# Gate and up of a SwiGLU feed-forward as seven block products, with summed weights made by accumulating DMAs

## The chip, the cores and the metric

The kernel runs on one NeuronCore of one Trainium2 chip. The metric is the device time of one execution in microseconds (us), lower is better. The core has five engines that run side by side, each in its own program order: TensorE (PE, matmuls; PEld is its weight load), VectorE (DVE), ScalarE (ACT), GpSimd (POOL) and SyncE (SP, which here only issues DMAs).

## What is computed

Two transformer blocks run one after the other on 256 tokens of 1024 channels, all in float32. The first has four layers (convolution, pooling, differential attention, convolution), the second two layers with a token mixer each. Eight SwiGLU feed-forwards (FFN) lie between them, one in each layer of the first block and two in each layer of the second:

```python
def _swiglu(xn, w_gate, w_up, w_down):
    return (jax.nn.silu(xn @ w_gate) * (xn @ w_up)) @ w_down
```

`xn` is 256 x 1024 (normalised), `w_gate` and `w_up` are 1024 x 2816, `w_down` is 2816 x 1024. The mixers between the feed-forwards are not touched by the change.

## The kernel before

**Split numbers.** A float32 operand is held as two fp32r tiles, a rounded high part and the low rest. `mm3` (L184 to L191) makes one 128-row product with three matmuls: high times high (L187), high times low (L188), low times high (L189). A weight block is loaded by SP from HBM into a slot of pool `r8` (L113), ACT rounds it into a second slot (L134) and DVE subtracts to get the low part in a third (L135), each in two halves of 128x1024. There are 19 such slots.

**The planner.** All weight loads stand in one list of pieces of up to 1 MB (`add`), in the order of their use. Every `mm3` ends with `tick`, which records at most one half of a split (`split_step`) and any delayed tasks that are due. `need(i)` forces the splits up to piece i, `done` frees the two slots of a piece, and `load_step` issues the next load when a slot is free. So the order on all engines comes from counting ticks (three matmuls each) while the program is recorded.

**The feed-forward.** `ffn` (L337) works on six chunks of the 2816 columns, five of 512 and one of 256. `gate_up(c, h)` takes one half h of the tokens (128) against gate and up of a chunk: for each of the two, eight blocks of 128 channels accumulate in a PSUM bank. ACT then takes SiLU of the gate (L368), DVE multiplies by up (L369), PE transposes the result four times (L375), ACT and DVE split it (L196, L197), and `down(c, h)` accumulates it against `w_down` into two banks per half. `chain` at the end of each half takes the norm, adds to x and transposes x for the next part (`post`, `scale_of`, `to_T`).

```python
    def tick(self):
        self.ticks += 1
        self.split_step()
        for t in list(self.tasks):
            if t in self.tasks and t[0] <= self.ticks:
                self.step(t)
```

Of the kernel before, what the change touches and what calls it, by code (L numbers as in the profile page):

```python
# [27 lines left out]
ORD = "VQKvco"  # L28

# [20 lines left out]
class Core:  # L50
    def __init__(self, ctx, tc, I, out):
# [21 lines left out]
        self.raw, self.hl, self.xt = {}, {}, {}  # L73
        self.raw_max = 3
        self.spare = 2
        self.hold = 0
        self.rr = {}
# [17 lines left out]
    def add(self, *srcs):  # L95

        self.pieces.append(srcs)
        return len(self.pieces) - 1

    def view(self, t, i):  # L100
        srcs = self.pieces[i]
        kt, n = srcs[0].shape[1], sum(s.shape[2] for s in srcs)
        return t[:, 0:kt * n].rearrange("p (k n) -> p k n", k=kt)

    def load_step(self, most=10 ** 9):
        while self.n_dma < most and self.n_dma < len(self.pieces) and len(self.r8.free) > self.spare and len(self.raw) < self.raw_max:
# [8 lines left out]
            self.raw[i] = t  # L115
            self.n_dma += 1

    def split_step(self, force=False, eng=None):
        i = self.n_split
        if i >= len(self.pieces):  # L120
            return False
        if self.sub == 0:
# [3 lines left out]
            if i not in self.raw:  # L126
                return False
            self.hl[i] = (self.r8.get(), self.r8.get())
            self.live += 1
        hi, lo = (self.view(t, i) for t in self.hl[i])  # L130
        k = lo.shape[1]
        sl = slice(0, k // 2) if self.sub == 0 else slice(k // 2, k)
        raw = self.view(self.raw[i], i)[:, sl]
        self.nc.scalar.copy(out=hi[:, sl], in_=raw)  # L134
        (eng or self.nc.vector).tensor_tensor(out=lo[:, sl], in0=raw, in1=hi[:, sl].bitcast(F32), op=ALU.subtract)  # L135
        self.sub += 1
        if self.sub == 2:
            self.sub = 0
            self.r8.put(self.raw.pop(i))
            self.n_split += 1  # L140
            self.load_step()
        return True

    def need(self, i):
        self.cur = max(self.cur, i)
        while self.n_split <= i:
            assert self.split_step(force=True), ("no buffer for piece", i, self.n_dma, self.n_split, len(self.raw), self.raw_max, len(self.r8.free), self.sub)
        return tuple(self.view(t, i) for t in self.hl[i])
# [35 lines left out]
    def mm3(self, out, x, w, first, last, tick=True):  # L184

        mm = self.nc.tensor.matmul
        mm(out=out, lhsT=x[0], rhs=w[0], start=first, stop=False)  # L187
        mm(out=out, lhsT=x[0], rhs=w[1], start=False, stop=False)  # L188
        mm(out=out, lhsT=x[1], rhs=w[0], start=False, stop=last)  # L189
        if tick:  # L190
            self.tick()  # L191
# [64 lines left out]
    def scale_of(self, h):  # L256
# [5 lines left out]
        def rest():  # L262
            r = self.sb.tile([128, 4], F32, tag=f"rr{h}", name=f"rr{h}", bufs=2)
            self.rstd(sx, 2, EPS, r)
            self.rr[h] = r[:, 1:2]
        return rest

    def to_T(self, h, gT, rest, late):
# [12 lines left out]
        for n, z in enumerate(zs):  # L281
            dst = [t[:, 0:2048].rearrange("p (k t) -> p k t", k=8)[:, 4 * n:4 * n + 4, h * 128:(h + 1) * 128] for t in self.xT]
            self.split(dst[0], dst[1], z.rearrange("p (k t) -> p k t", k=4))
            self.f2.put(z)
# [5 lines left out]
        self.spawn(last(), 3 if late else 0)  # L290
        yield
# [18 lines left out]
    def start(self, h, nxt, wait=None, late=False):  # L310
        rest = (lambda: self.scale_of(h)()) if late else self.scale_of(h)
# [4 lines left out]
        else:  # L316
            self.hold += 1
            self.xt[h] = self.spawn(self.to_T(h, self.gT, rest, late), 6 if wait is None else wait)


    def plan_ffn(self, wg, wu, wd):

        G, Dn = [], []
# [3 lines left out]
        for c in range(6):  # L327
            lo = c * 512
            if c < 5:
                G.append([self.add(w[:, 4 * q:4 * q + 4, lo:lo + 512]) for w in (gk, uk) for q in range(2)])  # L330
                Dn.append([self.add(dk[:, 4 * c + 2 * q:4 * c + 2 * q + 2, :]) for q in range(2)])
            else:
                G.append([self.add(gk[:, 4 * q:4 * q + 4, lo:lo + 256], uk[:, 4 * q:4 * q + 4, lo:lo + 256]) for q in range(2)])
                Dn.append([self.add(dk[:, 20:22, :])])
        return G, Dn

    def ffn(self, plan, half, nxt):  # L337
        G, Dn = plan
        self.limit = 6
# [3 lines left out]
        hT, tt = {}, {}  # L343

        def gate_up(c, h):
# [22 lines left out]
            self.nc.scalar.activation(out=s[:, 0:n], in_=gb, func=ACTF.Silu, scale=rr[h])  # L368
            self.nc.vector.scalar_tensor_tensor(out=s[:, 0:n], in0=ub, scalar=rr[h], in1=s[:, 0:n], op0=ALU.mult, op1=ALU.mult)  # L369
            self.ps.put(*banks)  # L370

            def T():
                b = self.ps.get()
                for j in range(n // 128):
                    self.nc.tensor.transpose(out=b[:, j * 128:(j + 1) * 128], in_=s[:, j * 128:(j + 1) * 128], identity=self.ident)  # L375
                self.f2.put(s)
                hT[c, h] = (self.r2.get(), self.r2.get())
                self.split(hT[c, h][0][:, 0:n], hT[c, h][1][:, 0:n], b[:, 0:n])
                self.ps.put(b)
                yield  # L380
            tt[c, h] = self.spawn(T(), 11 if c < 5 else 3)
# [25 lines left out]
        for c in range(5):  # L407
            if c == 4 and nxt == "pool":
                self.band = self.r8.get(F32)
                self.nc.sync.dma_start(out=self.band[:, 0:1568], in_=self.band_dram)  # L410
            gate_up(c, 0)
            if c:
                down(c - 1, 1)
            else:
# [1028 lines left out]
```

## Time and profile before

| | |
|---|---|
| median of 3 runs | 2160.31 us (2160.1 to 2162.17) |
| the profiled execution's own time | 2164.11 us |
| its span in the profile | 2162.3 us |
| mean granted TensorE clock | 0.997 |
| busy share of the span: PE, DVE, ACT, POOL | 99%, 57%, 49%, 4% |
| moved by DMA | 383.73 MB, 177 GB/s |

The profile is one execution, seen by engine. Busy time of an engine is the union of its instructions' times; matmuls are pipelined, so a matmul's duration (0.39 us) is longer than the step from one start to the next, and the step is what counts. "idle before" says how long an engine stood idle ahead of a group and which instruction ended that.

### The profile page before, as it was taken

Reading aid. Unit: us, or ns where it says so; the run is one execution under the profiler, and the core shown is the slowest. Engines: PE = TensorE matmul, PEld = TensorE weight load, DVE = VectorE, ACT = ScalarE, POOL = GpSimd, SP = SyncE. Lnnn points to the kernel's source line nnn. Section 1 sums busy time; section 2 is a strip of 40 time slices with the busy share of each in tenths; the row PEclk is TensorE's granted clock in tenths of the full one; section 3 lists DMA queues with packets and bytes.
Section 4 is the critical chain, followed back from the end, with each engine's and each line's share of the span. In section 5 each row is a group of like instructions: output and inputs, shape, how many; then the busy total and the mean of one; then the engine's idle time right before and its main releaser. Section 6 shows DMA issues by size and latency. Waiting matters only on the chain.

```text
span 2162.3 us, 24820 instructions
## 1 busy us (share of the span) xinstructions
PE 2138.5 (99%) x9845; PEld 1729.2 (80%) x9845; DVE 1237.1 (57%) x1664; ACT 1066.4 (49%) x1566; POOL 82.2 (4%) x130
## 2 busy tenths in 40 slices
PE   9999999999999999999999999999999999999998
PEld 6878877887888888888888887878888888787886
DVE  6655475546665456655464554785456446477454
ACT  5554454444664435553454446764435345676342
POOL 1000010000010000000000001000000001000000
PEclk9999999999999999999999999999999999999999
DMA  8555545455454554554654554354554645345541
GB/s 295 188 201 197 190 166 179 171 196 186 137 197 163 200 189 161 210 179 156 213 189 170 193 181 142 118 193 167 196 191 150 214 171 171 128 165 175 175 176 59
DMA packets 175620, 383.73 MB, mean 177 GB/s; under 512 B 10428, under 2 KB 29116, under 8 KB 175504
## 3 DMA queue, kind: packets, MB, share of 16 engines
q1 hardware_dynamic: 172592, 372.04, 50.2%
q0 software_dynamic: 2624, 9.58, 1.2%
q8 instruction: 77, 1.26, 0.2%
q10 hardware_dynamic: 288, 0.52, 0.1%
q14 instruction: 39, 0.32, 0.0%
HBM read 380.28 MB, written 1.84 MB: 177 GB/s over the span
## 4 chain that ended last, share of the span: by engine, by line
PE 93%; DVE 3%; ACT 2%; issue 1%; POOL 1%; DMA 0%; SPq 0%; POOLq 0%; DVEq 0%; ACTq 0%
PE ps L189 29%; PE ps L188 29%; PE ps L187 29%; PE ps L206 2%; PE ps L375 2%; ACT r L134 1%; DVE r L135 1%; PE ps L1042 1%; ACT c_junk L220 1%; PE ps L687 0%; PE ps L732 0%; PE ps L783 0%; PE ps L1016 0%; ACT f L1029 0%; DMA r<-in_conv_w_in_dram 0%
## 5 line engine op out<-in xcount | busy, mean ns | idle before, releaser
L187 PE MATMUL ps<-r,r 128*128 128x512 f32 (+2 forms) x2816 | 1129.5, 401 | 2.6 <-ACT r L196 1.7
L188 PE MATMUL ps<-r,r 128*128 128x512 f32 (+2 forms) x2816 | 1108.1, 394 | 2.5 <-POOL r L135 1.4
L189 PE MATMUL ps<-r,r 128*128 128x512 f32 (+2 forms) x2816 | 1109.5, 394 | 0.1
L135 DVE TENSOR_TENSOR r<-r,r 128x1024 fp32r<-128x1024 f32 (+1 forms) x701 | 815.1, 1216 | 147.0 <-ACT r L134 140.3
L134 ACT CAST r<-r 128x1024 fp32r<-128x1024 f32 x702 | 686.0, 1041 | 194.7 <-PE ps L188 166.8
L189 PEld LDWEIGHTS ps<-r,r 128*128 128x128 f32 (+1 forms) x2816 | 528.2, 188 | 127.1 <-DVE r L197 3.8
L188 PEld LDWEIGHTS ps<-r,r 128*128 128x128 f32 (+1 forms) x2816 | 529.3, 188 | 119.3 <-DVE r L135 3.0
L187 PEld LDWEIGHTS ps<-r,r 128*128 128x128 f32 (+1 forms) x2816 | 529.3, 188 | 118.8 <-ACT r L196 2.2
L369 DVE SCALAR_TENSOR_TENSOR f<-ps,rr,f 128x512 f32<-128x512 f32 (+1 forms) x96 | 67.8, 706 | 458.6 <-PE ps L189 434.4
L196 ACT CAST r<-ps 128x512 fp32r<-128x512 f32 (+1 forms) x108 | 59.9, 555 | 456.2 <-PE ps L375 448.1
L197 DVE TENSOR_TENSOR r<-ps,r 128x512 fp32r<-128x512 f32 (+1 forms) x108 | 70.2, 651 | 189.4 <-ACT r L196 189.4
L368 ACT ACTIVATE f<-ps,rr 128x512 f32<-128x512 f32 (+1 forms) x96 | 62.6, 653 | 156.9 <-PE ps L189 156.8
L216 POOL TENSOR_TENSOR st<-st,c_mhalf 128x1 f32<-128x1 f32 x28 | 15.9, 569 | 1575.7 <-DVE st L215 1574.9
L220 ACT ACTIVATE c_junk<-x 128x512 bf16<-128x512 f32 x56 | 35.3, 631 | 51.3 <-DVE x L253 50.2
L375 PEld LDWEIGHTS ps<-c_ident,f 128*128 128x128 f32 x352 | 44.4, 140 | 13.1
L375 PE MATMUL ps<-c_ident,f 128*128 128x128 f32 x352 | 54.0, 272 | 0.0
L277 DVE TENSOR_TENSOR f<-ps,c_pre 128x512 f32<-128x512 f32 x52 | 33.8, 687 | 29.5 <-PE ps L206 29.3
L196 ACT CAST r<-f 128x512 fp32r<-128x512 f32 x52 | 31.7, 621 | 26.1 <-DVE f L277 26.0
L253 DVE SCALAR_TENSOR_TENSOR x<-f,st,x 128x512 f32<-128x512 f32 x56 | 39.6, 749 | 2.5 <-POOL st L216 0.9
L245 DVE TENSOR_TENSOR f<-ps,gn 128x512 f32<-128x512 f32 x52 | 35.5, 684 | 6.4 <-ACT c_junk L220 6.4
L220 ACT ACTIVATE c_junk<-ps 128x512 bf16<-128x512 f32 x52 | 31.0, 596 | 15.2 <-PE ps L189 14.4
L197 DVE TENSOR_TENSOR r<-f,r 128x512 fp32r<-128x512 f32 x52 | 35.6, 722 | 4.6 <-ACT r L196 2.5
(177 smaller groups left out, 749.3 us busy)
## 6 DMA issues: line engine op xcount, KB each, us to landing
r<-in_ffn_w_in_dram SPq DMA_DIRECT2D x80, 1024.0 KB, 5.2
r<-in_ffn_w_down_dram SPq DMA_DIRECT2D x44, 1024.0 KB, 5.0
r<-in_ffn_w_out_dram SPq DMA_DIRECT2D x44, 1024.0 KB, 5.1
r<-in_ffn_w_gate_dram SPq DMA_DIRECT2D x40, 1024.0 KB, 5.1
r<-in_ffn_w_up_dram SPq DMA_DIRECT2D x40, 1024.0 KB, 5.1
r<-in_mix_w_in_dram SPq DMA_DIRECT2D x28, 1024.0 KB, 5.1
r<-in_conv_w_in_dram SPq DMA_DIRECT2D x22, 1024.0 KB, 5.3
r<-in_attn_w_qkv_dram SPq DMA_DIRECT2D x12, 1024.0 KB, 5.2
```

The costliest lines, as they stand in the source:

```text
L134: self.nc.scalar.copy(out=hi[:, sl], in_=raw)
L135: (eng or self.nc.vector).tensor_tensor(out=lo[:, sl], in0=raw, in1=hi[:, sl].bitcast(F32), op=ALU.subtract)
L187: mm(out=out, lhsT=x[0], rhs=w[0], start=first, stop=False)
L188: mm(out=out, lhsT=x[0], rhs=w[1], start=False, stop=False)
L189: mm(out=out, lhsT=x[1], rhs=w[0], start=False, stop=last)
L196: self.nc.scalar.copy(out=hi, in_=src)
L197: self.nc.vector.tensor_tensor(out=lo, in0=src, in1=hi.bitcast(F32), op=ALU.subtract)
L206: self.nc.tensor.transpose(out=b[:, j * 128:(j + 1) * 128], in_=src[:, j * 128:(j + 1) * 128], identity=self.ident)
L220: self.nc.scalar.activation(out=self.junk[:, 0:src.shape[-1]], in_=src, func=ACTF.Square, scale=scale, accum_out=acc)
L368: self.nc.scalar.activation(out=s[:, 0:n], in_=gb, func=ACTF.Silu, scale=rr[h])
L369: self.nc.vector.scalar_tensor_tensor(out=s[:, 0:n], in0=ub, scalar=rr[h], in1=s[:, 0:n], op0=ALU.mult, op1=ALU.mult)
L375: self.nc.tensor.transpose(out=b[:, j * 128:(j + 1) * 128], in_=s[:, j * 128:(j + 1) * 128], identity=self.ident)
```

## The change

Chunks 1 to 4 of each feed-forward (`SUMS`) no longer take `gate_up`. With two halves of the tokens, two halves of the input channels, and gate and up as the two column blocks, gate and up of a chunk are a 2x2 by 2x2 block product, which before was eight products of 12 matmuls. `seven(c)` takes seven: a11·b11, a12·b21, s1·t1, s2·t2, s4·b22, s3·t3, a22·t4. b11 and b21 are the upper and lower channel halves of gate, b12 and b22 those of up. The sums are t1 = b11 + b12, t2 = t1 + b22, t4 = t2 + b21 and t3 = b22 + b12. The sums of x (s1 to s4) are made once per feed-forward (`x_sums`, a task that follows the second `to_T`).

A summed block is made in place: when ACT and DVE have split the raw block, POOL issues a DMA that adds the next block from HBM onto the raw slot, and the sum is split in turn. In chunk 1 alone t1 is summed by DVE from two loaded blocks. A split of a summed block is not recorded earlier than 14 ticks (42 matmuls) after its DMA, unless it is forced. Loads, sums and splits of a chunk stand in a new order (`plan_ffn`), and each half's two `down` parts of the chunk before stand between the products.

```diff
+    def add_sums(self, b11, b12, b21, b22, loaded):
+        at = {}
+        def take(name):
+            src, more = {"b11": (b11, b12), "t1": (b11, b22), "t2": (b11, b21), "t4": (b11, None),
+                         "b22": (b22, b12), "t3": (b22, None), "b21": (b21, None)}[name]
...
+    def flush(self, keep=0):
+        while len(self.lows) > keep:
+            lo, raw, hi, eng, i, last = self.lows.popleft()
+            eng.tensor_tensor(out=lo, in0=raw, in1=hi.bitcast(F32), op=ALU.subtract)
+            if last:
+                self.n_low = i + 1
+                src, more, _ = self.units[i]
+                if more is None:
+                    self.r8.put(self.raw.pop(src))
+                elif more is not IN_PLACE:
+                    self.nc.gpsimd.dma_start(out=self.view(self.raw[src], src), in_=more, accum_op=ALU.add)
+                    self.due[src] = self.ticks + 14
...
         if self.sub == 0:
-            if not force and (self.hold or i > self.cur + self.ahead or self.live >= self.limit or len(self.r8.free) < 2):
+            if not force and (self.hold or i > self.cur + self.ahead or self.live >= self.limit or self.due.get(src, 0) > self.ticks
+                              or len(self.r8.free) < 2 + self.reserve):
...
+            if first is not None:
+                a, b = (self.view(self.raw[n], src) for n in (src, first))
+                self.nc.vector.tensor_tensor(out=a, in0=a, in1=b, op=ALU.add)
...
+        for c in SUMS:
+            if c > 1:
+                factors(c, "b21")
+            factors(c, "b22", "t2")
+            down(c - 1, 0)
+            factors(c + 1, "b11")
+            factors(c, "t3")
+            down(c - 1, 1)
+            factors(c, "t4")
+            factors(c + 1, "t1")
...
+        def seven(c):
...
+            product(X, "b11", "a11", True)
+            e1 = self.spawn(copy("1", X), 2)
+            product(Z, "b21", "a12", True)
+            self.join(e1)
+            e2 = self.spawn(gate0(), 2)
+            Y = self.ps.get()
+            product(Y, "t1", "s1", True)
+            e3 = self.spawn(copy("5", Y), 2)
+            product(X, "t2", "s2")
+            e4 = self.spawn(copy("2", X), 2)
+            down(c - 1, 0, (0,))
+            down(c - 1, 1, (0,))
+            self.join(e2, e3)
+            product(Y, "b22", "s4")
+            self.join(e4)
+            e5 = self.spawn(up0(), 2)
+            product(X, "t3", "s3")
+            e6 = self.spawn(up1(), 1)
+            down(c - 1, 0, (1,))
+            down(c - 1, 1, (1,))
+            self.join(e5, e6)
+            product(X, "t4", "a22")
```

`copy` is an ACT copy of a PSUM bank to SBUF, after which the bank goes on accumulating; `gate0`, `up0` and `up1` are one DVE addition of a bank and such a copy each, the first with SiLU on ACT behind it, the second with the DVE multiplication; `gate1` is SiLU and multiplication of the second half. Other edits: DVE's subtraction is recorded one split later than ACT's rounding, the negated row scale is kept for both halves, and live splits in a feed-forward may be 7 (6 before).

The order of POOL in the fifth feed-forward before: between its last small steps and those of the next part it has nothing (L216 are powers for the norms, L228 loads a gain, L902 belongs to the mixer).

```order
L216 TENSOR_TENSOR rr0_9186<-rr0_9186,c_mhalf_65 128x1
L216 TENSOR_TENSOR st4_9201<-st4_9201,c_mhalf_65 128x1
L228 DMA gn_1_9207<-in_norm_gain_2_dram 128x1024
L902 MEMSET r8_9_9233 128x768
L216 TENSOR_TENSOR rr1_9275<-rr1_9275,c_mhalf_65 128x1
```

The same engine now, from the start of the fifth feed-forward (L164 is the accumulating DMA, `r8_9_8420` is block b11 of chunk 2, `r8_11_8518` is b22 of chunk 2).

```order
L295 DMA gn_0_8220<-in_norm_gain_2_dram 128x1024
L283 TENSOR_TENSOR rr1_8263<-rr1_8263,c_mhalf_65 128x1
L164 DMA r8_7_8098<-in_ffn_w_in_2_dram 128x4x512
L164 DMA r8_11_8351<-in_ffn_w_in_2_dram 128x4x512
L164 DMA r8_7_8098<-in_ffn_w_in_2_dram 128x4x512
L164 DMA r8_9_8420<-in_ffn_w_in_2_dram 128x4x512 x2
L164 DMA r8_11_8518<-in_ffn_w_in_2_dram 128x4x512
L164 DMA r8_9_8420<-in_ffn_w_in_2_dram 128x4x512
```

There are 15 such DMAs of 1 MB in a feed-forward, three onto one block in turn.

The order of ACT in the same feed-forward, at the end of chunk 1 and the start of chunk 2 (`r8_13_8660` is the high part of t2 of chunk 2, L556 the SiLU of chunk 1's second half, L533 a copy of a bank, L263 the split of a transposed result).

```order
L201 CAST r8_13_8660<-r8_9_8420 128x1024
L556 ACTIVATE f2_1_8663<-ps_5_8415,rr1_8263 128x512
L201 CAST r8_13_8660<-r8_9_8420 128x1024
L201 CAST r8_15_8682<-r8_10_8554 128x1024 x2
L533 COPY f2_6_8690<-ps_3_8651 128x512
L263 CAST r2_0_8701<-ps_1_8696 128x512
```

The rounding of a summed block stands directly ahead of a SiLU that PE's next transposes depend on.

The order of DVE at the start of the same feed-forward (L380 to L387 are the sums of x, L187 the sum t1 of chunk 1, L157 the low part of a weight block, L510 the product of gate and up in chunk 0).

```order
L264 TENSOR_TENSOR r8_1_8281<-f2_9_8250,r8_16_8280 128x512
L157 TENSOR_TENSOR r8_14_8302<-r8_11_8273,r8_15_8301 128x1024 x2
L387 SCALAR_TENSOR_TENSOR f2_3_8192<-f2_6_8185,f2_3_8192 128x512
L264 TENSOR_TENSOR r8_1_8281<-f2_6_8185,r8_16_8280 128x512
L510 SCALAR_TENSOR_TENSOR f2_5_8329<-ps_2_8226,rr0_8198,f2_5_8329 128x512
L264 TENSOR_TENSOR r8_1_8281<-f2_3_8192,r8_16_8280 128x512
L187 TENSOR_TENSOR r8_7_8098<-r8_7_8098,r8_3_8118 128x2048
L157 TENSOR_TENSOR r8_12_8355<-r8_7_8098,r8_17_8354 128x1024 x2
```

The sums of x stand among the splits, and the first accumulating DMA (onto `r8_7_8098`) can only go out behind the last row here.

## Rows read from the trace of the kernel before

**Rows 1.** The page: busy time by engine, and the chain that ended last.
```profile
PE 2138.5 (99%) x9845; PEld 1729.2 (80%) x9845; DVE 1237.1 (57%) x1664; ACT 1066.4 (49%) x1566; POOL 82.2 (4%) x130
...
PE 93%; DVE 3%; ACT 2%; issue 1%; POOL 1%; DMA 0%; SPq 0%; POOLq 0%; DVEq 0%; ACTq 0%
PE ps L189 29%; PE ps L188 29%; PE ps L187 29%; PE ps L206 2%; PE ps L375 2%; ACT r L134 1%; DVE r L135 1%; PE ps L1042 1%; ACT c_junk L220 1%; PE ps L687 0%; PE ps L732 0%; PE ps L783 0%; PE ps L1016 0%; ACT f L1029 0%; DMA r<-in_conv_w_in_dram 0%
```

**Rows 2.** Busy time in four feed-forwards (us and instructions, clock, DMA share, GB/s).
```profile
925.20:1115.60 190.40, 190.40 (x854) 154.55 (x853) 103.15 (x112) 84.94 (x111) 3.82 (x5) 1.00 0.54 185
1115.60:1306.00 190.40, 190.33 (x854) 154.04 (x852) 101.61 (x111) 82.14 (x110) 6.62 (x10) 1.00 0.54 185
1452.60:1642.30 189.70, 189.70 (x848) 153.65 (x848) 101.79 (x110) 84.97 (x111) 2.74 (x5) 1.00 0.53 183
1642.30:1832.00 189.70, 189.70 (x848) 153.59 (x847) 101.61 (x111) 82.12 (x110) 6.16 (x9) 1.00 0.54 186
```

**Rows 3.** Timeline of PE in a feed-forward: start, us, instruction.
```profile
119.69 0.39 PE L188 MATMUL ps<-r,r 128*128 128x512 f32 x1
...
127.53 0.39 PE L189 MATMUL ps<-r,r 128*128 128x512 f32 x1
127.77 0.60 PE L375 MATMUL ps<-c_ident,f 128*128 128x128 f32 x4
128.12 0.47 PE L187 MATMUL ps<-r,r 128*128 128x512 f32 x1
...
133.05 0.39 PE L188 MATMUL ps<-r,r 128*128 128x512 f32 x1
...
138.42 0.39 PE L187 MATMUL ps<-r,r 128*128 128x512 f32 x1
```

**Rows 4.** Groups of instructions, whole span: busy us, mean ns, idle before.
```profile
L135 DVE TENSOR_TENSOR r<-r,r 128x1024 fp32r<-128x1024 f32 (+1 forms) x701 | 815.1, 1216 | 147.0 <-ACT r L134 140.3 <-PE ps L189 4.1
L134 ACT CAST r<-r 128x1024 fp32r<-128x1024 f32 x702 | 686.0, 1041 | 194.7 <-PE ps L188 166.8 <-DVE r L135 21.7 <-DMA r<-in_conv_w_in_dram 6.2
...
L197 DVE TENSOR_TENSOR r<-ps,r 128x512 fp32r<-128x512 f32 (+1 forms) x108 | 70.2, 651 | 189.4 <-ACT r L196 189.4
L369 DVE SCALAR_TENSOR_TENSOR f<-ps,rr,f 128x512 f32<-128x512 f32 (+1 forms) x96 | 67.8, 706 | 458.6 <-PE ps L189 434.4 <-ACT f L368 24.2
L368 ACT ACTIVATE f<-ps,rr 128x512 f32<-128x512 f32 (+1 forms) x96 | 62.6, 653 | 156.9 <-PE ps L189 156.8
...
L245 DVE TENSOR_TENSOR f<-ps,gn 128x512 f32<-128x512 f32 x52 | 35.5, 684 | 6.4 <-ACT c_junk L220 6.4
...
L689 ACT COPY f<-ps 128x512 f32<-128x512 f32 x20 | 11.6, 579 | 2.5 <-PE ps L687 2.4
```

**Rows 5.** DMA: queue's packets, MB, share; issues with KB and us to landing.
```profile
q1 hardware_dynamic: 172592, 372.04, 50.2%
...
r<-in_ffn_w_in_dram SPq DMA_DIRECT2D x80, 1024.0 KB, 5.2
...
r<-line POOLq DMA_DIRECT2D x1, 768.0 KB, 5.0
```

**Rows 6.** Busy time of a stretch with loads waiting in the queue.
```profile
20.00:30.00 10.00, 10.00 (x45) 8.08 (x44) 9.15 (x10) 9.26 (x13) 1.78 (x3) 1.00 1.05 402
```

**Rows 7.** Timeline of POOL: a DMA of 128x4x384.
```profile
137.23 0.79 POOL L654 DMA_DIRECT2D r<-line  x1 [3.02 <-DMA line<-f]
```

**Rows 8.** Timeline of DVE at the start of the fifth feed-forward.
```profile
1109.47 1.29 DVE L197 TENSOR_TENSOR r<-f,r 128x512 fp32r<-128x512 f32 x2
1110.68 0.21 DVE L215 TENSOR_SCALAR rr<-st 128x1 f32<-128x1 f32 x1
1111.01 6.90 DVE L135 TENSOR_TENSOR r<-r,r 128x1024 fp32r<-128x1024 f32 x6
1117.83 0.74 DVE L369 SCALAR_TENSOR_TENSOR f<-ps,rr,f 128x512 f32<-128x512 f32 x1
1124.20 0.69 DVE L197 TENSOR_TENSOR r<-ps,r 128x512 fp32r<-128x512 f32 x1 [5.62 <-ACT r L196]
```

More of the change, by code (lines that the diff above doesn't have):

```diff
@@ L134, in split_step @@
         self.nc.scalar.copy(out=hi[:, sl], in_=raw)
[L135 to L141, printed above, removed]
+        self.lows.append((lo[:, sl], raw, hi[:, sl], eng or self.nc.vector, i, self.sub == 1))
+        self.flush(1)
+        self.n_split += self.sub
@@ L265, in rest, with to_T @@
             self.rr[h] = r[:, 1:2]
+            if neg:
+                self.nc.vector.tensor_scalar(out=r[:, 2:3], in0=r[:, 1:2], scalar1=-1.0, scalar2=None, op0=ALU.mult)
+                self.nr[h] = r[:, 2:3]
         return rest
-    def to_T(self, h, gT, rest, late):
+    def to_T(self, h, gT, rest, late, keep=False):
         if h == 0:
@@ L290, in to_T, with x_sums, put @@
         self.spawn(last(), 3 if late else 0)
+        if keep and h:
+            self.st = self.spawn(self.x_sums(), 2)
+        yield
+    def x_sums(self):
+        tt, stt = self.nc.vector.tensor_tensor, self.nc.vector.scalar_tensor_tensor
+        while len(self.r8.free) < 2:
+            yield 1
+        self.xs = (self.r8.get(), self.r8.get())
+        self.reserve = 0
+        z = self.z
+        def put(j, t):
+            self.split(self.xs[0][:, j * 512:(j + 1) * 512], self.xs[1][:, j * 512:(j + 1) * 512], t)
+        tt(out=z[1, 1], in0=z[1, 1], in1=z[1, 0], op=ALU.subtract)
+        tt(out=z[1, 0], in0=z[0, 0], in1=z[1, 0], op=ALU.subtract)
+        put(0, z[1, 1])
+        yield 3
+        stt(out=z[0, 0], in0=z[1, 1], scalar=-1.0, in1=z[0, 0], op0=ALU.mult, op1=ALU.subtract)
+        put(3, z[1, 0])
+        yield 3
+        stt(out=z[0, 1], in0=z[0, 0], scalar=-1.0, in1=z[0, 1], op0=ALU.mult, op1=ALU.subtract)
+        put(1, z[0, 0])
+        yield 3
+        put(2, z[0, 1])
+        self.f2.put(*z.values())
+        z.clear()
         yield
@@ L338, in ffn @@
         G, Dn = plan
-        self.limit = 6
+        nc = self.nc
+        self.limit, self.reserve, self.ahead = 7, 2, 4
         self.join(self.xt[0])
@@ L343, in ffn, with hidden, T @@
         hT, tt = {}, {}
+        def hidden(s, c, h, n, delay):
+            def T():
+                while not self.ps.free or len(self.r2.free) < 2:
+                    yield 1
+                b = self.ps.get()
+                for j in range(n // 128):
+                    nc.tensor.transpose(out=b[:, j * 128:(j + 1) * 128], in_=s[:, j * 128:(j + 1) * 128], identity=self.ident)
+                self.f2.put(s)
+                hT[c, h] = (self.r2.get(), self.r2.get())
+                self.split(hT[c, h][0][:, 0:n], hT[c, h][1][:, 0:n], b[:, 0:n])
+                self.ps.put(b)
+                yield
+            tt[c, h] = self.spawn(T(), delay)
         def gate_up(c, h):
@@ L367, in gate_up @@
             s = self.f2.get()
[L368 to L369 removed]
+            nc.scalar.activation(out=s[:, 0:n], in_=gb, func=ACTF.Silu, scale=rr[h])
+            nc.vector.scalar_tensor_tensor(out=s[:, 0:n], in0=ub, scalar=rr[h], in1=s[:, 0:n], op0=ALU.mult, op1=ALU.mult)
             self.ps.put(*banks)
[L372 to L379, printed above, removed]
[L380 removed]
```

185 lines of the change are left out of this document (144 added, 41 removed).

## The prediction, on record before the change was run

> **What bounds the kernel now.** I read the page first, for the busy shares and the chain of work that ended last: PE is busy 99% of the span and 93% of the chain is PE, nearly all of it the three lines of the split product [rows 1]. So time goes only where PE has fewer matmuls to run, or comes where PE has to wait. Then the busy time by stretch, over four feed-forwards: the first and the third window run from the first SiLU of one feed-forward to that of the next. One takes 190 us, PE has no gap in it, the clock is 1.00 (the 2.4 GHz level), DVE is busy 102 us of it, ACT 84, the DMA engines 0.54 [rows 2]. The reader is to see that all three have room, and how much. Then PE's timeline, for the step from one matmul to the next, which the duration of 0.39 us hides: 34 steps from 119.69 to 127.53 are 0.2306 us each, 23 steps from 133.05 to 138.42 with ACT and DVE at work are 0.2335 [rows 3]. I take 0.232. Four transposes put 0.35 us between two matmuls [rows 3]. As a test: 792 matmuls of a feed-forward (96 in each of five chunks, 48 in the sixth, 264 in `down`) x 0.232 = 183.7 us, with 15 groups of transposes (11 of results, 4 of x) 5.3 us more: 189, against the 190 measured.
>
> **What it removes.** A chunk's gate and up are 96 matmuls before and 7 x 12 = 84 now. 12 x 4 chunks x 8 feed-forwards = 384 matmuls of 512 columns go, and the transposes stay. At 0.232 us that is 89.1 us, 11.1 for each feed-forward, which would take 179. This is the whole gain; everything below is what may be given back.
>
> **What it adds on ACT and DVE.** In each feed-forward 12 more blocks are split (seven for four, four times): 24 roundings x 1.041 and 24 subtractions x 1.216 us [rows 4]. ACT also gets 12 copies of a bank x 0.579 and 4 roundings of sums of x (about 0.6): 25.0 + 6.9 + 2.4 = 34 us, so 84 + 34 = 118 of 179 us, 66%. DVE gets 12 additions with a bank (0.684, the nearest row is the product of a bank and a gain), 8 operations on sums of x (0.7), and t1 of chunk 1 over 2048 columns (two of 1.216): 29.2 + 8.2 + 5.6 + 2.4 = 45, so 102 + 45 = 147 of 179 us, 82%. Inside one of the middle chunks PE has 132 matmuls and two groups of transposes, 31.3 us. DVE has 18 subtractions, 3 additions, 2 products (0.706) and 2 splits (0.651): 26.7 us, 85%. Neither engine becomes the bound by its sum. What they cost is delay: a bank has to be copied or added before PE writes it again. The tightest is `up1`, recorded one tick into the eight that `down` gives PE between t3 and t4: 21 matmuls, 4.9 us, for about two queued subtractions (2.4) and the addition (0.7). It fits, with little over. I charge 0.4 us a chunk for misses (between 0 and 1.5), 1.6 a feed-forward.
>
> **The start of a feed-forward.** Here DVE already works without a pause from 1111.01 to 1118 in the trace of before, and idles 5.6 us soon after [rows 8]. The sums of x and t1, 8 us, now go in between, and five blocks are split ahead of chunk 1 (12.2 us). About 21 us of DVE work stand in 18 us of PE time, so DVE comes out some 3.5 us late. Behind it wait the first accumulating DMA and with it t2 of chunk 1. PE wants t2 63 matmuls (14.6 us) after the place where that DMA is recorded; less the split of its first half (1.04 + 1.22) 12.3 us remain, against 3.5 late + 0.8 on POOL + the landing (below, 7.8) = 12.1. I charge 2 us (0.5 with a landing like a plain one, 4 with a longer one).
>
> **The accumulating DMAs.** No row of before has one. 15 x 1 MB in each feed-forward, and three loads of weights fewer, so 45 transfers for 33. The price has two sides. Engine time: a stretch with loads waiting moves 402 GB/s at a DMA share of 1 [rows 6], so 1.0486 MB takes 2.61 us. A middle chunk has 5 loads and 4 accumulations: at the price of a load (the lower end) 9 x 2.61 = 23.5 us of 31.3, at twice that, since the sum must be read as well as the source, (5 + 8) x 2.61 = 33.9 us, over PE's time. Landing: a load lands 5.2 us after its issue, and one of 768 KB issued by POOL after 5.0 [rows 5], so 5.2 is the lower end and 5.2 + 2.6 = 7.8 what a second reading adds; 10.4 is the upper end. POOL takes 0.79 us to issue such a shape [rows 7], 120 of them are 95 us on an engine that is busy 82 [rows 1]. I take the double price for the landing and something between one and two for the engines, because the nearest row is a transfer that reads the same bytes once.
>
> Who waits: the split of a sum is recorded 42 matmuls (9.7 us) or more after its DMA. ACT stands in order, so a late landing holds all that is behind the rounding; at the head of a chunk that is SiLU of the chunk before, whose transposes PE reaches 18 matmuls (4.2 us) on. Rounding, SiLU (0.653) and product need 2.4 of these, so 9.7 + 1.8 = 11.5 us are covered, against 1.5 of DVE's delay + 0.8 + 7.8 = 10.1. So they cost nothing while they land within 9.2 us of issue; beyond that PE stands once a chunk for what is over. For the engines, a small excess is borrowed from the two or so transfers that are asked for ahead (about 5 us).
>
> The Trainium skill speaks against this part. Collectives: The Full Stack, "The bandwidth ceiling: the fold count and why AG ≠ RS ≠ AR", says that adding in the DMA path reads two sources on one ring and moves about half of what a copy does (32.35 GB/s to 62.28); by that ratio, 1.93, a middle chunk would keep the DMA engines busy for an estimated 33.2 us, and the sum would be 0.7 us a feed-forward worse. No row of before shows it.
>
> **Other edits.** SP issues three loads fewer a feed-forward; one that finds no slot free holds those behind it, as before, and they are asked for 24 matmuls (5.6 us) or more ahead of their split against a landing of 5.2: nothing while the engines have room. Seven splits may live instead of six and a subtraction is recorded one split later: nothing, PE uses a block many matmuls after it. POOL's powers for the norms come behind the last accumulation of a feed-forward, which is issued over a chunk earlier: nothing. `down`'s results are transposed a few ticks after SiLU as before. The mixers keep their order.
>
> **Sum.** A feed-forward gives 11.1 - 2 - 1.6 = 7.5 us, eight give 60. Against the profiled execution's own 2164.1 us that is 2104, and the median of the runs lies 3.8 us under that execution: 2100.
>
> **Rivals.** *All hidden:* neither the start nor the chunks cost anything; 2160 - 89 = 2071, to 2083 with a small loss. For it speaks the gapless PE in [rows 2]; against it DVE at 82%. *The vector engine sets the pace:* its queue delays the banks, 1.5 us in each of 32 chunks and 4 at each of 8 starts, 80 us: 2151. The point from which it decides is a delay of DVE over about 3 us in mid chunk; for it speaks that it has 85% there, against it that subtractions have no one close behind them. *The DMA engines set the pace* (the other side): if an accumulation takes 2.5 times a load's engine time, a middle chunk needs (5 + 10) x 2.61 = 39.2 us, 7.9 over PE's; three such chunks less 5 borrowed are 18.6 us, with the 3.6 above 22.2 lost for 11.1 won: 11.1 x 8 = 89 slower, 2249. It decides from about 2.15 loads on, where the chunk takes 35.5 us. For it speaks the second reading on engines that would be 0.75 busy without it; against it the room from 0.54 [rows 2]. The Trainium skill's page named above puts the ratio just below that point. That fewer matmuls are run is read from the order itself and can't fail.
>
> **How the numbers follow.** Forecast (2083 to 2130) 0.58; all hidden 0.10; vector engine (2130 to 2156) 0.12; within 0.2% (4.3 us, about what a measurement of this kernel can tell from no change) 0.03, where losses happen to meet the gain; DMA engines 0.17, half of it under 2220. The range runs from 2072 to 2185: below it lies little, above it most of the DMA rival, some 0.13 together. Faster 0.58 + 0.10 + 0.12 = 0.80, same 0.03, slower 0.17.
>
> **What would show it.** Right: some 9460 PE instructions instead of 9845; the step still 0.231 to 0.234; feed-forwards of 181 to 184 us; DVE near 147 and ACT near 118 us in one; accumulations that land in 7 to 9 us; the DMA share near 0.75; PE's gaps in the first 20 us of chunk 1. Wrong: PE idle in mid chunk ended by ACT or DVE behind a rounding of a summed block (landing over 9 us, or a share near 1), PE waiting on `up1` or `gate0`, or a step above 0.236.

## The result, and the profile after

The changed kernel is slower: 2429.65 us (2428.47 to 2437.95, 4 runs) against 2161.24 us (2160.1 to 2163.1, 4 runs) of the kernel before, a ratio of 1.1249 with a 95% interval from 1.1223 to 1.1276. Forecast were 2100 us, in a range from 2072 to 2185. Line numbers from here on are those of the changed kernel or of the run named: L254 to L256 are the three matmuls of a product, L478 the transposes of a result, L201 the rounding of a block, L157 its low part, L164 the accumulating DMA, L533 the copy of a bank, L543 and L545 addition and product of `up0`. In the kernels with accumulating DMAs in fewer chunks, lines that come later in the file are 9 further on: L487 are the transposes, L542 the copy, L554 the product of `up0`, L567 that of `gate1`.

The page of the profile after, first the engines, then the DMA queues (packets, MB, share of 16 engines), POOL's issue (mean ns) and the issues with KB and us to landing:

```profile
PE 2145.4 (88%) x9461; PEld 1713.0 (70%) x9461; DVE 1573.8 (65%) x2040; ACT 1319.8 (54%) x1886; POOL 232.6 (10%) x250
...
q1 hardware_dynamic: 159920, 346.88, 40.6%
q0 software_dynamic: 65984, 135.42, 30.0%
...
L164 POOL DMA_DIRECT2D r<-in_ffn_w_in_dram x60 | 77.1, 1285 | 550.4 <-DVE r L157 541.0
...
r<-in_ffn_w_in_dram SPq DMA_DIRECT2D x68, 1024.0 KB, 7.7
r<-in_ffn_w_in_dram POOLq DMA_DIRECT2D x60, 1024.0 KB, 14.0
...
r<-in_ffn_w_up_dram POOLq DMA_DIRECT2D x44, 1024.0 KB, 13.7
```

PE runs the 9461 instructions expected in place of 9845 [rows 1], but its share falls from 99 to 88%. A sum lands 14 us after its issue, a plain load 7.7 instead of 5.2 [rows 5]. The waits, with total, count and longest, say who stands for that:

```profile
ACT r L201 <- DMA r<-in_ffn_w_in_dram: 287.0, 57, 11.5
ACT r L201 <- DMA r<-in_ffn_w_up_dram: 248.9, 41, 11.3
...
PE ps L478 <- DVE f L545: 171.8, 32, 7.9
...
PE ps L254 <- ACT f L533: 76.7, 17, 8.6
```

ACT waits over 500 us for transfers; before, 6.2 us [rows 4]. PE itself waits, in the rows above, not for a rounding but for the transposes' input and for copies of banks. Two middle chunks of the fifth feed-forward, SiLU to SiLU (columns as in [rows 2]), and the DMA engines in 40 slices of the second:

```profile
1320.90:1361.80 40.90, 33.88 (x140) 27.30 (x140) 25.29 (x25) 21.24 (x26) 5.12 (x4) 0.87 0.92 229
1361.80:1403.80 42.00, 34.55 (x144) 27.77 (x143) 25.29 (x25) 21.35 (x27) 5.13 (x4) 0.88 0.92 230
```

```profile
DMA  9999999999999999999999999930000049999999
```

A chunk takes 41 to 42 us where its matmuls and transposes need 31.3. The DMA engines are busy 0.92 of it, and yet they idle for some 5 us, from about 1390 on. The timelines of POOL, ACT, DVE and PE there show why both can be:

```profile
1371.85 1.28 POOL L164 DMA_DIRECT2D r<-in_ffn_w_in_dram  x1 [4.69 <-PE ps L256]
1393.90 1.28 POOL L164 DMA_DIRECT2D r<-in_ffn_w_in_dram  x1 [20.77 <-DVE r L157]
```

```profile
1380.73 2.00 ACT L201 CAST r<-r 128x1024 fp32r<-128x1024 f32 x2 [3.11 <-DMA r<-in_ffn_w_in_dram]
1388.77 4.83 ACT L201 CAST r<-r 128x1024 fp32r<-128x1024 f32 x5 [6.04 <-DMA r<-in_ffn_w_in_dram]
```

```profile
1389.85 1.23 DVE L157 TENSOR_TENSOR r<-r,r 128x1024 fp32r<-128x1024 f32 x1 [5.68 <-ACT r L201]
1390.99 0.68 DVE L543 TENSOR_TENSOR f<-ps,f 128x512 f32<-128x512 f32 x1
1391.71 0.75 DVE L545 SCALAR_TENSOR_TENSOR f<-f,rr,f 128x512 f32<-128x512 f32 x1
```

```profile
1384.76 0.40 PE L256 MATMUL ps<-r,r 128*128 128x512 f32 x1
1392.61 1.09 PE L478 MATMUL ps<-c_ident,f 128*128 128x128 f32 x4 [7.45 <-DVE f L545]
1393.35 0.78 PE L254 MATMUL ps<-r,r 128*128 128x512 f32 x1
1393.92 0.63 PE L255 MATMUL ps<-r,r 128*128 128x512 f32 x1
1394.35 0.63 PE L256 MATMUL ps<-r,r 128*128 128x512 f32 x1
```

Read it from the top. The sum issued at 1371.85 is rounded at 1388.77, 16.9 us later. DVE's low part of it stands ahead of `up0`, so `up0`, whose banks had been ready, comes at 1390.99; the transposes follow at 1392.61, 7.45 us late. The next sum may go only when a low part is out, 22 us after the one before, and SP sends no load between 1378.60 and 1398.29 either, so the DMA engines run dry. And after the stop PE's next steps are 0.43 us apart instead of 0.23: the lower of its two clock levels.

Where the time went, counted from the starts of PE's matmuls in both traces, each interval by what it has beyond a step of 0.232 us: 384 steps fewer, -89 us; intervals of 0.8 us and more 74 instead of 11, 310.9 us instead of 18.2, which is +278 beyond the steps in them; 333 more steps between 0.38 and 0.5 us, +65; 32 more between 0.5 and 0.8 us, +12; the shorter ones +9. Together some 274, the difference of the spans of 2436.2 and 2162.3 us. The trace grants PE the lower clock in 319 of the 362 slow steps.

What the landing depends on shows in the same trace. First the view of L164, for the whole run:

```profile
DMA to landing us min/median/max: 8.4/13.8/17.7
```

Counted from the issues and landings in the trace, 24 of the 120 sums went out with no other transfer in flight and landed after 8.75 us in the median; 87 found two or more in flight and took 14.33.

### The profile page after: what moved, and what is told of

The parts are those of the page before. It is cut to its first block, busy times and chain, and to the rows that moved or that the text cites. A ratio compares the mean times of both kernels' runs of the same rounds, so it can differ in the third digit from the quotient of the medians.

```text
span 2436.2 us, 25161 instructions
## 1 busy us (share of the span) xinstructions
PE 2145.4 (88%) x9461; PEld 1713.0 (70%) x9461; DVE 1573.8 (65%) x2040; ACT 1319.8 (54%) x1886; POOL 232.6 (10%) x250
## 3 DMA queue, kind: packets, MB, share of 16 engines
q0 software_dynamic: 65984, 135.42, 30.0%
## 5 line engine op out<-in xcount | busy, mean ns | idle before, releaser
L157 DVE TENSOR_TENSOR r<-r,r 128x1024 fp32r<-128x1024 f32 x893 | 1050.4, 1216 | 491.2 <-ACT r L201 488.6
L201 ACT CAST r<-r 128x1024 fp32r<-128x1024 f32 x894 | 882.4, 1042 | 629.4 <-DMA r<-in_ffn_w_in_dram 287.0
L254 PE MATMUL ps<-r,r 128*128 128x512 f32 (+2 forms) x2688 | 1114.5, 415 | 79.9 <-ACT f L533 76.7
L255 PE MATMUL ps<-r,r 128*128 128x512 f32 (+2 forms) x2688 | 1087.0, 404 | 15.0 <-DVE r L157 13.6
L256 PE MATMUL ps<-r,r 128*128 128x512 f32 (+2 forms) x2688 | 1084.0, 403 | 0.0
L254 PEld LDWEIGHTS ps<-r,r 128*128 128x128 f32 (+1 forms) x2688 | 525.4, 195 | 204.3 <-ACT f L533 85.7
L256 PEld LDWEIGHTS ps<-r,r 128*128 128x128 f32 (+1 forms) x2688 | 521.7, 194 | 128.0 <-DVE r L264 4.0
L478 PE MATMUL ps<-c_ident,f 128*128 128x128 f32 x352 | 67.0, 318 | 181.3 <-DVE f L545 171.8
L478 PEld LDWEIGHTS ps<-c_ident,f 128*128 128x128 f32 x352 | 48.5, 162 | 205.6 <-issue 148.0
L164 POOL DMA_DIRECT2D r<-in_ffn_w_in_dram x60 | 77.1, 1285 | 550.4 <-DVE r L157 541.0
L558 DVE SCALAR_TENSOR_TENSOR f<-f,rr,f 128x512 f32<-128x512 f32 x32 | 24.0, 751 | 124.1 <-ACT f L556 123.9
L263 ACT CAST r<-ps 128x512 fp32r<-128x512 f32 (+1 forms) x108 | 59.7, 553 | 71.0 <-PE ps L478 60.3
L164 POOL DMA_DIRECT2D r<-in_ffn_w_up_dram x44 | 56.6, 1287 | 408.8 <-DVE r L157 324.5
L263 ACT CAST r<-f 128x512 fp32r<-128x512 f32 x84 | 51.5, 621 | 48.2 <-DVE f L347 22.0
L264 DVE TENSOR_TENSOR r<-f,r 128x512 fp32r<-128x512 f32 x84 | 57.4, 708 | 6.4 <-ACT r L263 4.3
L533 ACT COPY f<-ps 128x512 f32<-128x512 f32 x96 | 55.8, 581 | 0.0
L509 ACT ACTIVATE f<-ps,rr 128x512 f32<-128x512 f32 (+1 forms) x32 | 18.6, 580 | 57.0 <-PE ps L256 57.0
L539 ACT ACTIVATE f<-f,rr 128x512 f32<-128x512 f32 x32 | 23.2, 725 | 47.9 <-DVE f L537 47.9
## 6 DMA issues: line engine op xcount, KB each, us to landing
r<-in_ffn_w_down_dram SPq DMA_DIRECT2D x44, 1024.0 KB, 10.6
r<-in_ffn_w_up_dram POOLq DMA_DIRECT2D x44, 1024.0 KB, 13.7
```

Source lines behind the costliest of these rows:

```text
L157: eng.tensor_tensor(out=lo, in0=raw, in1=hi.bitcast(F32), op=ALU.subtract)
L164: self.nc.gpsimd.dma_start(out=self.view(self.raw[src], src), in_=more, accum_op=ALU.add)
L254: mm(out=out, lhsT=x[0], rhs=w[0], start=first, stop=False, skip_group_check=more)
L255: mm(out=out, lhsT=x[0], rhs=w[1], start=False, stop=False, skip_group_check=more)
L256: mm(out=out, lhsT=x[1], rhs=w[0], start=False, stop=last, skip_group_check=more)
L263: self.nc.scalar.copy(out=hi, in_=src)
```

## The experiments

Two theories stood against each other. **Engine time:** an accumulating DMA keeps the DMA engines busy for so long that a chunk can't be shorter than its transfers. **Landing and order:** a sum lands later than the order of the program allows for, and what stands in order behind its rounding on ACT, and behind its low part on DVE, is what PE waits for.

**What the transfers cost in all.** First plain writes for the sums, then those with a second transfer of the same size, then none (the calls are shortened; all three kernels leave out the addition).

```
plain writes     gpsimd.dma_start(out=raw, in_=more)
and a second     gpsimd.dma_start(out=raw, in_=more); gpsimd.dma_start(out=scratch, in_=more)
none             no transfer; 14 ticks kept
```

> Leaves out the additions: the 120 DMAs of POOL overwrite the raw block with the next one and don't add to it, everything else stays. Theory A (an accumulation takes the DMA engines 5.9 us, two loads' worth, and four of them with five loads fill a middle chunk): at a load's price of about 3 us the chunk has 27 us of DMA work for 31.3 us of PE, so the middle chunks fall from 41 to 31 to 33 us and the total to 2085 to 2130. Theory B (the place of the split is too near to its DMA, whatever the DMA costs): a plain write lands in about 6 us, inside the 9.7 us left for it, so B expects the same here. Theory C (ACT and DVE have too much to do or PE lost its clock for another reason): 2350 or more, since their work is unchanged.

> Leaves out the additions as the run with plain writes does, and adds to each of the 120 writes a second plain copy of the same 1 MB into scratch memory in HBM that nobody waits for. So the DMA engines have two transfers' work for each sum as with accumulation (about 38 us in a middle chunk of 31.3 us of PE), but no reading of the destination. Theory A (engine time): middle chunks of 38 to 42 us and a total of 2330 to 2450. Theory B (the landing of an accumulation is slow by itself and holds ACT): the plain write lands sooner than the sum did, chunks of 32 to 35 us, total 2100 to 2200.

> Leaves out the sums of weights altogether: the 120 accumulating transfers are gone (125.8 MB less is read), the second, third and fourth roundings of a block read it as it was. All instructions of the engines stay, as do the 14 ticks. What is left against the kernel before is the saving of 384 matmuls and whatever the engines themselves lose. Reading 'transfers alone': the 84 us of stops that the run with plain writes still had were waits for those writes too, so they go, and the time is 2075 to 2105 us. Reading 'engines too': the start of a feed-forward (sums of x on VectorE, copies of banks behind roundings on ScalarE) loses by itself what the run with plain writes showed there, about 6 to 8 us of each of 8 feed-forwards, and the time is 2120 to 2150 us, with the stops of 1.8 and about 4 us at the first sums still in the trace.

Measured, one run each: 2154.29 us with plain writes, 2295.84 with the second transfer, 2083.91 with none; 2429.65 with the sums. Without transfers the change wins 2161.43 - 2083.91 = 77.5 us of the 89, so all that the engines pay (12 more splits, copies, sums of x, the order) is some 12 us: the failure lies with the transfers and with what waits for them. 120 plain ones cost 70 us, a second one for each another 142, and the accumulation 134 beyond that. Plain writes stay 24 us above the 2085 to 2130 that both theories gave, by the loss at the start shown below; the run with a second transfer lies between the two ranges on record, so neither theory alone gives its time; the run with none lies in the range of "transfers alone".

The page gives the engine time: on q0 each sum takes (30.0 - 1.1)% of 2436.2 us over 120 = 5.87 us, with plain writes the same sum gives 2.96 (q0 at 17.6%, span 2152.5). The 1.1% is the queue's other traffic, as the run on GpSimd below has it alone. A write and its second transfer come by the same sum to 5.37 us (q0 at 29.2%, span 2293.9), close to an accumulation. So the sums keep the engines busy only 120 x 0.5 = 60 us longer in all, against 134 us of time; the other difference is the landing of what the rounding waits for, 10.5 us for the write and 14.0 for the sum. How the 134 divide was not tried. Queue and landing with the second transfer, then with plain writes alone, and PE's largest wait there:

```profile
q0 software_dynamic: 67904, 261.25, 29.2%
...
r<-in_ffn_w_in_dram POOLq DMA_DIRECT2D x60, 1024.0 KB, 10.5
```

```profile
q0 software_dynamic: 35264, 135.42, 17.6%
...
r<-in_ffn_w_in_dram POOLq DMA_DIRECT2D x60, 1024.0 KB, 7.0
```

```profile
PE ps L254 <- ACT f L533: 37.1, 8, 6.6
```

A landing of 7.0 us, close to the forecast's 7.8, costs nothing in a middle chunk: there the SiLU of tile 1 comes every 31 to 33 us (once 34), close to the 31.3 that PE needs. Most of the loss of 70 us lies at the start of a feed-forward, with one long wait in each of the eight: the copy that t2's bank needs stands behind a rounding that waits for the first of these writes. Another 10.6 us are waits for `up0`, nearly all in the last chunk with sums.

**Order alone, four chunks.** `self.due[src] = self.ticks + 28` for 14.

> The change with one number altered: the split of a sum is held back 28 ticks (84 matmuls, 19.5 us) after its DMA where nothing forces it, 14 before. Theory B (only the place of the split is wrong): ACT no longer waits 3 to 7 us at a time for sums, PE's stop of 8.6 us in each chunk goes, total 2130 to 2250. Theory A (DMA engine time): the chunk can't be shorter than its 38 us of DMA work, so 2350 to 2450, about as the change.

Measured 2387.61 us. The wait for copies and for `up0` is gone, but PE now waits for the roundings themselves:

```profile
PE ps L254 <- ACT r L201: 127.2, 33, 10.1
PE ps L255 <- DVE r L157: 76.0, 70, 1.8
```

Chunks stay at about 40 us. The time lies in the range of theory A, engine time: with neighbouring chunks all summed, holding the rounding longer gains 42 us of 268.

**Half the sums, then order.** `SUMS = (2, 4)`, the other chunks as eight products; then the same with 28 ticks.

> Seven products in chunks 2 and 4 alone, chunks 1 and 3 with eight as before the change; loads and splits in the order of use. Two chunks then have 11 loads and 4 accumulations, 11 x 3.0 + 4 x 5.9 = 57 us of DMA work in 65.4 us of PE time. Theory A: the engines have room on average, the total falls below the kernel before by up to 45 us less the losses: 2115 to 2165. Theory B (the split stands too near to its DMA): a stop of some 5 to 8 us remains in each of the 16 chunks with sums, total 2200 to 2250.

> Sums in chunks 2 and 4 only, as in the run of 2293.8 us, and 28 ticks instead of 14 between issue and rounding. The DMA engines have room here: a chunk with sums and one without are 9 to 10 loads of 2.61 us and 4 sums of 5.85 us, some 50 us of some 65. Reading 'engine time': only the DMA engines' load matters, which is unchanged, so 2280 to 2310 us. Reading 'landing and order': the stops are copies of banks and products that stand on ScalarE and VectorE behind the rounding of a sum that has not landed; with 28 ticks sums land first, the 84 us of stops on copies of banks and the steps at the low clock behind them fall below 20 us, and the time is 2150 to 2220 us. A third way: matmuls wait for the late roundings themselves, as they did with 28 ticks in all four chunks (127 us there), and the time is 2270 to 2330 us with the stops at matmuls behind ScalarE's roundings of weights.

Measured 2293.76 us, a ratio of 1.062 (1.0601 to 1.0639), and 2166.02, a ratio of 1.0021 (1.0012 to 1.003). The DMA load is the same in both (q0 18.2 and 19.0%, sums landing after 10.5 to 11.3 us), and 128 us lie between them: with room on the engines, how long the rounding is held, and so what stands behind it, decides. The first lies above both ranges on record, the second in that of "landing and order". The wait that went is the first row (14 ticks), what is left the second (28):

```profile
PE ps L254 <- ACT f L542: 83.9, 27, 8.9
```

```profile
PE ps L255 <- DVE r L157: 26.0, 29, 1.5
```

**The sums on GpSimd.** Chunks 2, 3 and 4; all four blocks are loaded by SP; `gpsimd.tensor_tensor(out=a, in0=a, in1=b, op=add)` makes each sum.

> Seven products in chunks 2, 3 and 4 (24 feed-forward chunks, 288 matmuls or 66.8 us less than before), no accumulating transfer: all four blocks of a chunk are loaded whole by SP and added on GpSimd, four additions of 128x2048 a chunk, and the sums of x are made in the time of chunk 1 instead of at the start. Estimate of an addition from the 128x1024 tensor operations on GpSimd in the trace of before, 2.36 us each: 4.7 us, 19 us of a chunk of 31. Reading 'the accumulating transfer was the fault': 2095 to 2130 us, middle chunks of 31 to 33 us. Reading 'the engines do not carry seven products in any case' (copies behind roundings, VectorE, or GpSimd in VectorE's way): 2150 to 2220 us, chunks of 34 us and more.

Measured 2433.14 us, a ratio of 1.1252 (1.1234 to 1.1271): as slow as the change, without one accumulating DMA. An addition takes 5.04 us in the mean, near the estimate, but VectorE stands while GpSimd adds. Timelines of POOL and of DVE, and the roundings that wait for additions (L149 the addition, L180 the low part, L219 the rounding there):

```profile
1125.68 10.13 POOL L149 TENSOR_TENSOR r<-r,r 128x2048 f32<-128x2048 f32 x2 [3.60 <-DVE r L180]
```

```profile
1126.67 10.23 DVE L180 TENSOR_TENSOR r<-r,r 128x1024 fp32r<-128x1024 f32 x2
...
1147.07 2.34 DVE L180 TENSOR_TENSOR r<-r,r 128x1024 fp32r<-128x1024 f32 x2
```

```profile
ACT r L219 <- POOL r L149: 303.3, 54, 10.7
```

Two subtractions take 10.23 us beside two additions and 2.34 alone, and roundings wait up to 10.7 us for a sum, about as long as for a transfer. So the first reading, 2095 to 2130, falls; the second has the right cause, but with 2150 to 2220 priced it at less than a quarter of the 272 us. How the loss divides between held subtractions and roundings that wait wasn't tried. The Trainium skill, SBUF — State Buffer, "Who interferes with whom", says that a VectorE instruction with two inputs in SBUF contends with a GpSimd instruction that reads SBUF, and that one of them blocks; the trace agrees with 10.23 us for 2.34, and the expectation had named it in its second reading without a price. This run closes a way round; the slow time of the change itself is explained by the other runs.

**How long to hold a rounding, and where the sums of x stand.** Two chunks; 20, 24 and 28 ticks; the last three runs also begin the sums of x 20 ticks after the transposes:

```
-            self.st = self.spawn(self.x_sums(), 2)
+            self.st = self.spawn(self.x_sums(), 20)
...
-        self.join(self.st)
...
             if c in SUMS:
+                self.join(self.st)
                 seven(c)
```

> Sums in chunks 2 and 4 only, 20 ticks instead of 28. With 28 the second and third sums of a block were rounded only when their product was already due, and TensorE stood about 1.2 us for the low part in each (2 stops a chunk, 16 chunks); with 20 ticks, 13.9 us at 0.232 us a step, their roundings come 12 to 45 steps ahead of the product, and a transfer that lands 11 to 12.5 us after its low part is out is down. Reading 'landing and order': 32 stops of 1.2 us go, minus 0.2 us each that a stop shorter than a step hides, so 2125 to 2145 us. Reading 'the landing is longer than 13.9 us where it matters': stops on copies of banks come back, 2165 to 2230 us.

> As the run with 20 ticks, and the sums of x are begun 20 ticks after the transposes instead of 2, in the time of chunks 0 and 1. The start of a feed-forward showed stops of 1.84 and 1.2 us that TensorE spent on VectorE there. Reading 'VectorE's sums of x delay the low parts of chunk 0': these two stops go, 2 to 3 us of each of 8 feed-forwards, so 16 to 24 us below the run with 20 ticks. Reading 'they only move to chunk 1': within 6 us of it. The saving worked out for 16 chunks is 192 matmuls or 44.5 us below the kernel before, 2116 us; nothing should come out below 2112.

> Sums in chunks 2 and 4, sums of x in the time of chunks 0 and 1, and 24 ticks (16.7 us at 0.232 us a step). With 20 ticks the one stop left in each chunk with sums was 3.3 to 4.2 us at the transposes of the first token tile, which wait for VectorE's product, which stands behind the low part of the fourth sum, whose transfer has not landed; with 28 that stop was not there, but the roundings came when their product was due. With 24 the fourth sum is rounded 24 steps later than with 20, behind that product in the order of the program, and still 21 steps ahead of its own use. Reading 'landing and order': both kinds of stop are gone, 2112 to 2130 us, faster than the kernel before by 1.5 to 2.2 per cent. Reading 'engine time': the load on the DMA engines is the same as with 20 ticks, so 2180 to 2200 us.

> As the run with 28 ticks (2166 us), with the sums of x in the time of chunks 0 and 1. That move took 46 us off with 20 ticks. If what it takes away is the start of the feed-forward and nothing else, it takes as much off here: 2116 to 2135 us; the two stops of 1.2 us a chunk behind low parts that come too late stay. If with 28 ticks the start is hidden otherwise, 2150 to 2170 us.

Measured against 2162.28 and 2161.37 us: 20 ticks 2240.36, a ratio of 1.0363 (1.0349 to 1.0377); 20 with late sums of x 2194.12, 1.0159 (1.0143 to 1.0174); 24 with late sums 2164.22, 1.0015 (1.0006 to 1.0024); 28 with late sums **2133.84 us, 0.9872 (0.9858 to 0.9885), 1.3% faster than the kernel before**. Moving the sums of x took 46 us off with 20 ticks, twice what was expected (PE's intervals of 0.8 us and more fall from 62 to 35), and 32 with 28. The first readings for 20 and for 24 ticks fell, both by a stop of some 2 to 4 us in nearly every chunk with sums. With 20 it is again `up0` behind the low part of a sum, so 13.9 us were too short:

```profile
PE ps L487 <- DVE f L554: 48.4, 15, 3.8
```

With 24 that is over, and the stop is at the last product's transposes, for another reason. PE's largest wait with 24 ticks, then DVE's and PE's timelines:

```profile
PE ps L487 <- DVE f L567: 28.5, 16, 2.1
```

```profile
1262.77 9.16 DVE L157 TENSOR_TENSOR r<-r,r 128x1024 fp32r<-128x1024 f32 x8
1271.85 0.75 DVE L567 SCALAR_TENSOR_TENSOR f<-f,rr,f 128x512 f32<-128x512 f32 x1
```

```profile
1270.70 0.39 PE L256 MATMUL ps<-r,r 128*128 128x512 f32 x1
1272.66 0.66 PE L487 MATMUL ps<-c_ident,f 128*128 128x128 f32 x4 [1.57 <-DVE f L567]
```

Splits are made in order, so those behind the held one pile up and then go out in a row: eight low parts, 9.16 us, ahead of the product. With 28 ticks fewer of them stand ahead of the last product, five or six instead of seven to nine, and the stop there is gone. DVE's timeline with 28:

```profile
1243.53 5.77 DVE L157 TENSOR_TENSOR r<-r,r 128x1024 fp32r<-128x1024 f32 x5 [0.26 <-ACT r L201]
1249.21 0.75 DVE L567 SCALAR_TENSOR_TENSOR f<-f,rr,f 128x512 f32<-128x512 f32 x1
```

Intervals of 0.8 us and more come to 37.0 us instead of 60.9, and 33 steps fewer are slow, 0.2 us each: some 30 us, the difference of the two times (the profiled spans differ by 27.3). 8.5 us of it is one stop in a mixer that runs into the first feed-forward: its copy of a bank on ACT stands behind a rounding that waits 8.71 us for a sum, and with 28 ticks it does not. With 28 PE's busy share is 98%, and one wait for low parts is left, 15.5 us:

```profile
PE 2098.5 (98%) x9653; PEld 1686.7 (79%) x9653; DVE 1417.1 (66%) x1888; ACT 1199.5 (56%) x1742; POOL 160.6 (8%) x194
...
q0 software_dynamic: 36416, 76.69, 19.5%
```

```profile
PE ps L255 <- DVE r L157: 15.5, 20, 1.3
```

Of 192 matmuls, 44.5 us, 27.5 are won.

**Three chunks in a row** with 24 ticks: `SUMS = (2, 3, 4)`.

> As the run with 24 ticks, but with sums in chunks 2, 3 and 4, three in a row. The program order is mended; what is left against it is the load on the DMA engines, 5 loads of 2.61 us and 4 sums of 5.85 us a chunk, 36.5 us, against 31.3 us of matmuls and transposes. Reading 'engine time bounds neighbouring chunks': chunks of 36 us and more, which gives back what the third chunk saves (2.8 us) and more, 2150 to 2230 us, slower than with chunks 2 and 4. Reading 'only landing and order matter': one more chunk saved, 22 us below the run with 24 ticks, 2090 to 2110 us.

Measured 2241.71 us, a ratio of 1.0384 (1.0366 to 1.0402): 77 us slower than with two chunks, where the third saves 22, and 12 above the range of "engine time". PE's largest wait, chunks 2, 3 and 4 of a feed-forward, then ACT's timeline in the third:

```profile
PE ps L254 <- ACT r L201: 66.0, 17, 8.1
```

```profile
1199.34:1239.48 40.14, 40.14 (x179) 32.53 (x178) 24.82 (x26) 21.41 (x26) 5.10 (x4) 1.00 1.04 283
1239.48:1277.57 38.09, 34.04 (x137) 26.59 (x136) 24.06 (x25) 20.62 (x26) 4.37 (x4) 0.91 0.96 236
1277.57:1320.75 43.18, 35.56 (x148) 28.05 (x147) 24.52 (x26) 21.36 (x26) 3.32 (x3) 0.88 0.82 211
```

```profile
1291.30 2.94 ACT L201 CAST r<-r 128x1024 fp32r<-128x1024 f32 x3 [6.84 <-DMA r<-in_ffn_w_in_dram]
```

The DMA engines are full through two chunks (1.04, 0.96); the first (still with matmuls of its neighbour in the window) loses nothing, the second 4 us; in the third a rounding waits 6.84 us for a sum, and PE 7.1 for that rounding. So the engines have no room left in the first two, which fits "engine time". With 0.82 in the third they were not always what was waited for; how its loss divides between load and order stays open.

## Why the prediction was wrong

**Right:** the saving (9461 instructions; without transfers 77.5 us of 89.1 came out); the step (0.23 us wherever the clock was full); ACT and DVE: busy time grew by 253.4 / 8 = 31.7 and 336.7 / 8 = 42.1 us a feed-forward, against 34 and 45 forecast. "0.4 us a chunk" and "2 us" for the start more than cover what the engines cost by themselves: 3.6 us a feed-forward forecast, (89.1 - 77.5) / 8 = 1.5 measured. The vector engine was no bound. That a landing of up to 9.2 us is covered in a middle chunk is borne out for the 7.0 and 7.3 of plain writes; whether it holds up to 9.2 no run shows.

**The step that failed** is the one on the accumulating DMAs: "So they cost nothing while they land within 9.2 us of issue", with 7.8 us taken for the landing. Four things were wrong.

- The landing: 14.0 and 13.7 us, beyond even the upper end of 10.4. The bounds came from loads in a queue with room [rows 5]. For a sum with no other transfer in flight they were nearly right: 8.75 us, under the 9.2 that are covered. With two or more in flight it was 14.33. Landing and load were priced one by one, and the one makes the other.
- The engine time: "something between one and two" loads of 2.61 us. Measured 5.87 us, 2.25 of them, past the point of 2.15 from which the text itself let the DMA engines decide, and 1.98 plain transfers of POOL at 2.96. The Trainium skill, Collectives: The Full Stack, "The bandwidth ceiling: the fold count and why AG ≠ RS ≠ AR", gives 1.93 by its bandwidths for collectives; the runs agree with it, with 1.98 for these sums. By it the prediction came to 0.7 us a feed-forward, because the excess was to be borrowed from transfers asked for ahead; with the order holding the next sum back there was nothing to borrow from. The forecast charged nothing for the engines, though 1.5 loads, the middle of its own bounds, already fill (5 + 6) x 2.61 = 28.7 of 31.3 us, a share of 0.92; the 0.75 among the signs of being right goes with the price of one load, 23.5 us.
- What stands behind: the text knew that ACT stands in order, and covered SiLU at the head of a chunk. It passed over `up0` behind a low part on DVE, and over copies of banks behind roundings that wait. Those are the two waits of the profile, 171.8 and 76.7 us, 248.5 of the 278 us of stops.
- The start: 2 us, at most 4. Plain writes that land after 7 us already cost 70 / 8 = 8.8 us a feed-forward, most of it there.

**The rival** on the DMA engines had the right side, at 0.17, and the wrong size. By its own formula a price of 2.25 loads gives chunks of (5 + 9) x 2.61 = 36.5 us, 3 x 5.2 - 5 + 3.6 = 14 us lost for 11.1 won, 25 us slower or 2185. The 245 us beyond that are chunks of 41 us in which DMA work and waiting follow each other, the start, and some 65 us of slow steps, nearly all at the lower clock level, which no term had.

The prediction's own signs of being wrong came true: a landing over 9 us, a share near 1 (0.92), and PE idle in mid chunk behind DVE and ACT.

## What to carry to other kernels

Where a kernel adds in place by DMA, price the transfer as here at two plain ones on the DMA engines, and its landing at what it takes with others in flight (14.33 us), not alone (8.75); then look on every in-order engine at what stands behind the instruction that waits for it, low parts and products included, not only at its user. Sums in every second chunk, rounded only when they have landed and with the sums of x moved out of the start, are worth having (27.5 us here); sums in every chunk turn a gain of 89 us into a loss of 268, and of 226 with 28 ticks. No run moves `up0` itself ahead of the low part that holds it, so what four chunks could give in a better order stays open. Where holding work back makes what follows pile up, move the holder, and read the queue again: 20, 24 and 28 ticks differed by 60 us with the same transfers and the same work on every engine.

## What the runs showed of the hardware that was not expected

- After a wait of 7.45 us PE's matmuls came 0.43 us apart until 1397.34, 4 us later, before they went back to 0.23; the granted clock of that chunk was 0.88. In the run with 28 ticks and late sums of x, whose stops behind low parts are at most 1.3 us, it was 0.998 over the whole run. In the changed kernel the slow steps add 65 us to 278 us of stops.
- A sum of 1 MB with no other transfer in flight lands after 8.75 us in the median (24 of 120), a plain write of POOL after 5.63 (29 of 120); with two or more in flight after 14.33 and 7.94.
- GpSimd's addition of two blocks in SBUF holds VectorE's subtraction nearly for its whole length: 10.23 us for two, against 2.34.
- POOL issues an accumulating DMA of 1 MB in 1.285 us and a plain one in 0.752 (plain writes); the forecast took 0.79. An accumulation also runs as twice as many packets: (65984 - 2624) / 120 = 528, against (35264 - 2624) / 120 = 272.
